# Keeping split weights in DRAM and loading them whole in later groups of a hybrid encoder step

## The chip, the cores and the metric

The kernel runs on one core of a Trainium2 chip. The metric is the device time of one execution in microseconds (us), given as the median of several runs. Engines are named as the profile names them: PE (TensorE, its weight loads apart as PEld), DVE (VectorE), ACT (ScalarE), POOL (GpSimd) and SP (SyncE, which here issues nearly all DMAs).

## The reference, cut to what matters

Two layers are applied to 2048 prompt tokens and to 8 x 16 sample tokens. Each layer is one combined projection, two mixers (A, windowed attention; B, a gated linear attention), an output projection and a gated per-layer embedding.

```
u  = rms_norm(h) @ w_in            # split into qa, ka, va, ga, qb, kb, vb, gb, ab
oa = window attention of rope(norm(qa)), rope(norm(ka)), va     # with sinks
ob = gated linear attention of qb, kb, vb, gates from ab
mix = concat(oa * silu(ga), rms_norm(ob) * silu(gb))
h  = h + mix @ w_out
h  = h + sigmoid(rms_norm(h) @ w_pg) * (p_l @ w_pe)
```

All data are float32. The weights of a layer are the same for every token.

## The kernel before

**Groups.** The 17 tiles of 128 tokens are cut into five groups of 3, 4, 4, 3 and 3 tiles (n = 384 or 512 tokens). For each layer the five groups are gone through in turn: `phase_in` makes the projections and both mixers, `phase_out` the output projection and the gate. A group is called l0g3 for layer 0, group 3. Group 4 of each layer holds the sample tile.

**Three products for one.** A float32 matrix product is made of three matmuls on rounded operands (float32r): high x high, high x low, low x high (`mm3`, lines 394 to 404; its matmuls are L400, L401 and L402). So each weight has to be in SBUF twice, as a rounded high part and a low remainder. The high part is an ACT copy (L217), the low part a DVE subtraction (through the helper `ptt`, which is why its line is L96). This is done anew in every group, ten times over the program for groups and layers together, though the parts of one layer are the same in all five groups.

**Blocks, pieces, slots.** `plan` lists the weight blocks of a group in the order in which PE uses them: kv, q, ga0, ga1, qb, kb, vb, gb, then o0 to o3 (columns of w_out), then g0, e0, g1, e1, g2, e2, g3, e3 (w_pg and w_pe). A block is loaded in pieces of 256 KB (`w_dma`, L197, on SP's queue, into four `raw` buffers), and each piece is split by one ACT and one DVE instruction (`w_split`) into a slot. A slot of tag w is 1 MB: two pieces, high and low. There are five such slots (`RING`), so a group's 76 w-pieces go through them 38 slots one after another; the small e blocks have two slots of their own. A group has 80 pieces, the program 800.

**What sets the order.** `w_split` returns without work when all five slots are held. `freed` (called behind the matmuls of the last unit that uses a slot) gives a slot back and calls `w_split` again, and `w_ahead` does so ahead of each unit. So a slot is refilled as soon as PE has let go of its last user, in the order of `plan`. Raw pieces run four ahead of the splits. Every engine runs its instructions in the order in which the scheduler of the framework put them, so a split that waits on ACT or DVE holds back what stands behind it there. Attention and the linear attention are generators that `pump` steps between the dense units. The tail of `phase_in` is the part that is asked about below: after the last unit of block gb (L1055 to 1080 of the kernel) the linear attention of the last tiles is still open, with `gsq` (squares on ACT, L895), `gss` (their norm on POOL, L896 and L898), `on` (DVE, L901), the transposes of `on` on PE (L912), and `at` and `ke` (DVE L885, ACT L888), which PE waits for in `gla_prompt`; meanwhile PE has the first halves of o0 to o2 to do.

Of the kernel before, what the change touches and what calls it, by code (L numbers as in the profile page):

```python
# [8 lines left out]
F32 = mybir.dt.float32  # L9
# [37 lines left out]
def hybrid_step(ctx: ExitStack, tc: tile.TileContext, a: dict, o: dict):  # L47
    nc = tc.nc
    V, A, G, PE, SP = nc.vector, nc.scalar, nc.gpsimd, nc.tensor, nc.sync
# [4 lines left out]
    dram = ctx.enter_context(tc.tile_pool(name="dram", bufs=1, space=bass.MemoryType.DRAM))  # L54
# [40 lines left out]
    def ptt(out, in0, in1, op1, eng=None):  # L95
        (eng or G).tensor_tensor(out=out, in0=in0, in1=in1, op=op1)  # L96
# [45 lines left out]
    plan = []  # L142
    for l in range(DEPTH):
        for gi in range(len(GROUPS)):
# [8 lines left out]
            for b in range(4):  # L153
                plan.append((l, gi, f"g{b}", 8, [a["w_pg"][l, :, b]], 4, "w"))
                plan.append((l, gi, f"e{b}", 2, [a["w_pe"][l, :, b]], 2, "we"))
    RING = dict(w=5, we=2)
    pieces = []
    for bi, (_, _, _, K, srcs, ks, _) in enumerate(plan):
        for k0 in range(0, K, 2):
            c0 = 0  # L160
            for src in srcs:
                wd = src.shape[2]
                pieces.append((bi, k0 // ks, k0 % ks, c0, wd, src[:, k0:k0 + 2, :]))
                c0 += wd
    first_piece = {}
    last_piece = {}
# [6 lines left out]
    st = dict(dma=0, split=0, blk=0)  # L173
    wgate = [None]
    RAW = Z["raw"]
# [17 lines left out]
    def w_dma(upto):  # L193
        while st["dma"] < min(upto, len(pieces)):
            bi, _, _, _, wd, src = pieces[st["dma"]]
            r = w_p.tile([128, 2, wd], F32, tag="raw", name="raw", bufs=RAW)
            SP.dma_start(out=r, in_=src)  # L197
            raws[st["dma"]] = r
            st["dma"] += 1

    def w_split():
        i = st["split"]
        if i >= len(pieces):
            return False
        bi, si, kk, c0, wd, _ = pieces[i]
        _, _, _, _, srcs, ks, tag = plan[bi]
        if (bi, si) not in slots:
            if held[tag] == RING[tag]:
                return False
            held[tag] += 1  # L210
            slots[bi, si] = w_p.tile([128, 2, ks, sum(x.shape[2] for x in srcs)], F32R, tag=tag, name="w", bufs=RING[tag])
        w_dma(i + RAW)
        w = slots[bi, si]
        r = raws.pop(i)
        hi, lo = (w[:, x, kk:kk + 2, c0:c0 + wd] for x in range(2))
        with tc.issue_after(wgate[0]) if wgate[0] is not None else ExitStack():
            A.activation(out=hi, in_=r, func=ACTF.Copy)  # L217
        ptt(lo, r, hi, ALU.subtract, V)
        st["split"] += 1
        w_dma(i + 1 + RAW)  # L220
        return True

    def w_get(l, gi, nm):
        bi = st["blk"]
        assert plan[bi][:3] == (l, gi, nm), (plan[bi][:3], l, gi, nm)
        while st["split"] <= last_piece[bi]:
            assert w_split()
        st["blk"] += 1
        return Block(bi)

    def w_get_part(l, gi, nm):

        bi = st["blk"]
        assert plan[bi][:3] == (l, gi, nm), (plan[bi][:3], l, gi, nm)
        while st["split"] < first_piece[bi] + 2:
            assert w_split()
        st["blk"] += 1
        return Block(bi)

    def w_rest(w):  # L240
        while st["split"] <= last_piece[w.bi]:
            assert w_split()
# [95 lines left out]
    def prep_x(pool, l, gi, slot, out, whole=False):  # L338
# [6 lines left out]
        if whole:  # L345
            full = pool.tile([128, KD, n], F32, tag="hfull", name="hfull", bufs=1)
            for k in range(0, KD, 2):
                HQ[k // 2].dma_start(out=full[:, k:k + 2, :], in_=src[:, k:k + 2, t0:t0 + n])
                if k // 2 in WD:
                    w_dma(WD[k // 2])  # L350
# [85 lines left out]
    def phase_in(l, gi, ip, xn, mslot, S_in):  # L436
# [651 lines left out]
        for mt in range(4):  # L1088
            if mt == 3:
                with tc.issue_after(lastmm[0]):  # L1090
                    done["tail"]()
            pss.append(unit_a(mixes, ws[mt // 2], mt % 2, 0, n, pm(n) if mt < 2 else pw1(n), ks=(0, 4), end=mt % 2 == 1))
        ws.append(w_get_part(l, gi, "o2"))
        for mt in (4, 5):
            pss.append(unit_a(mixes, ws[2], mt % 2, 0, n, pw1(n), ks=(0, 4), end=mt % 2 == 1))
# [176 lines left out]
def _prepare(inputs):  # L1272
# [65 lines left out]
    for t in range(NT):  # L1338
# [18 lines left out]
             ks=(DEPTH, 128, 128), vs=(DEPTH, 128, 128), ss=(DEPTH, 8, 128, 2, 128))  # L1357
# [32 lines left out]
```

## Time and profile before

| | |
|---|---|
| median of 3 runs | 2314.01 us (2313.35 to 2318.27) |
| the profiled execution, its own time | 2322.44 us |
| its span, first to last instruction | 2320.7 us |
| mean granted TensorE clock | 0.993 |
| PE busy | 2268.3 us, 98% |
| DVE busy | 1605.0 us, 69% |
| ACT busy | 1272.2 us, 55% |
| DMA | 278.93 MB, mean 120 GB/s |

The profiled execution is 8.4 us longer than the median of the runs. Matmuls overlap in their records (one of 384 columns lasts 0.33 us and the next starts 0.17 us after it), so "busy" says that PE always had one under way. Idle time that the profile gives for PE is time with none under way.

### The profile page before, as it was taken

How to read it: one execution, taken by the hardware profiler on the slowest of the kernel's cores; microseconds unless marked ns; L12 is line 12 of the kernel's file. 1: busy time of each engine (PE TensorE's matmuls, PEld its weight loads, DVE VectorE, ACT ScalarE, POOL GpSimd, SP SyncE). 2: the span in 40 equal slices, each digit the busy share in tenths (PEclk: the TensorE clock that was granted, in tenths of full speed). 3: DMA queues.
4: the chain of work that ended last, by engine and by line, in shares of the span. 5: the costliest groups of instructions: out<-in, count | busy, mean ns of one | idle time of the engine just before them, and what ended most of it. 6: DMA issues, size and time to landing. Idle time of an engine off the chain costs nothing.

```text
span 2320.7 us, 40960 instructions
## 1 busy us (share of the span) xinstructions
PE 2268.3 (98%) x14814; PEld 1953.6 (84%) x14814; DVE 1605.0 (69%) x3279; ACT 1272.2 (55%) x2962; POOL 671.0 (29%) x771
## 2 busy tenths in 40 slices
PE   8999999999999999999999999999999999999999
PEld 7889877887788989987988998778877888798889
DVE  7767765767567766776777677657676678677755
ACT  6555644655455645654665566445555556566533
POOL 3124322342223231413322241314412142233222
PEclk9999999999999999999999999999999999999999
DMA  5344313433154425444543543244322443264343
GB/s 159 101 150 133 107 55 119 143 105 91 55 155 120 128 85 169 147 118 127 180 128 91 171 136 90 68 128 133 114 73 74 146 146 110 85 184 146 104 131 102
DMA packets 160234, 278.93 MB, mean 120 GB/s; under 512 B 17648, under 2 KB 43632, under 8 KB 160032
## 3 DMA queue, kind: packets, MB, share of 16 engines
q1 hardware_dynamic: 159344, 275.43, 39.4%
q8 instruction: 117, 1.92, 0.3%
q10 hardware_dynamic: 688, 0.88, 0.1%
q14 instruction: 85, 0.70, 0.1%
HBM read 255.41 MB, written 20.71 MB: 119 GB/s over the span
## 4 chain that ended last, share of the span: by engine, by line
PE 83%; ACT 4%; DVE 4%; DMA 4%; issue 3%; POOL 2%; ACTq 0%; DVEq 0%; POOLq 0%; SPq 0%
PE mm L400 15%; PE mm L402 15%; PE mm L401 14%; PE pw L400 9%; PE pw L401 9%; PE pw L402 9%; PE o L131 3%; DVE w L96 2%; PE s L131 2%; PE s L125 2%; DMA raw<-in_w_pe_dram 1%; DMA raw<-in_w_out_dram 1%; PE o L125 1%; ACT gsq L895 1%; ACT w L217 1%
## 5 line engine op out<-in xcount | busy, mean ns | idle before, releaser
L96 DVE TENSOR_TENSOR w<-raw,w 128x512 fp32r<-128x512 f32 (+1 forms) x800 | 571.7, 743 | 164.6 <-ACT w L217 161.7
L217 ACT ACTIVATE w<-raw 128x512 fp32r<-128x512 f32 (+1 forms) x800 | 468.9, 627 | 271.1 <-DMA raw<-in_w_pe_dram 60.0
L96 POOL TENSOR_TENSOR ot<-gth,hst 128x384 f32<-128x384 f32 (+1 forms) x79 | 101.7, 1291 | 287.6 <-DVE gth L1189 263.4
L400 PE MATMUL mm<-B,w 128*128 128x384 f32 (+1 forms) x440 | 160.8, 365 | 1.1 <-DVE yq L470 0.8
L402 PE MATMUL mm<-B,w 128*128 128x384 f32 (+1 forms) x440 | 159.8, 363 | 0.0
L401 PE MATMUL mm<-B,w 128*128 128x384 f32 (+1 forms) x440 | 159.0, 361 | 0.0
L400 PE MATMUL pw<-mix,w 128*128 128x384 f32 (+1 forms) x424 | 153.0, 361 | 0.0
L580 ACT ACTIVATE P<-s,mx 128x192 f32<-128x192 f32 (+3 forms) x272 | 108.8, 413 | 77.5 <-DVE mx L575 71.3
L401 PE MATMUL pw<-mix,w 128*128 128x384 f32 (+1 forms) x424 | 151.2, 357 | 0.0
L402 PE MATMUL pw<-mix,w 128*128 128x384 f32 (+1 forms) x424 | 151.0, 356 | 0.0
L400 PE MATMUL mm<-A,w 128*128 128x384 f32 (+1 forms) x408 | 148.5, 364 | 2.0 <-DVE yq L470 1.8
L96 POOL TENSOR_TENSOR acc<-sq,acc 128x384 f32<-128x384 f32 (+1 forms) x60 | 74.1, 1235 | 257.1 <-ACT sq L331 257.1
L402 PE MATMUL mm<-A,w 128*128 128x384 f32 (+1 forms) x408 | 148.0, 363 | 0.0
L401 PE MATMUL mm<-A,w 128*128 128x384 f32 (+1 forms) x408 | 147.8, 362 | 0.0
L400 PE MATMUL mm<-w,A 128*128 128x512 f32 (+1 forms) x360 | 138.2, 384 | 0.0
L400 PE MATMUL mm<-w,B 128*128 128x512 f32 (+1 forms) x360 | 137.9, 384 | 0.0
L402 PE MATMUL mm<-w,B 128*128 128x512 f32 (+1 forms) x360 | 137.7, 383 | 0.0
L402 PE MATMUL mm<-w,A 128*128 128x512 f32 (+1 forms) x360 | 137.6, 382 | 0.0
L401 PE MATMUL mm<-w,A 128*128 128x512 f32 (+1 forms) x360 | 137.4, 382 | 0.0
L401 PE MATMUL mm<-w,B 128*128 128x512 f32 (+1 forms) x360 | 137.4, 382 | 0.0
L96 POOL TENSOR_TENSOR mix<-ga_t,mix 128x512 fp32r<-128x512 f32 x34 | 43.9, 1290 | 283.1 <-ACT mix L606 283.1
L1186 ACT ACTIVATE gth<-gth 128x384 f32<-128x384 f32 (+2 forms) x81 | 45.1, 560 | 125.6 <-DVE gth L1185 125.3
(325 smaller groups left out, 6367.6 us busy)
## 6 DMA issues: line engine op xcount, KB each, us to landing
raw<-in_w_in_dram SPq DMA_DIRECT2D x400, 256.0 KB, 2.9
raw<-in_w_out_dram SPq DMA_DIRECT2D x160, 256.0 KB, 3.1
raw<-in_w_pg_dram SPq DMA_DIRECT2D x160, 256.0 KB, 2.9
raw<-in_w_in_dram SPq DMA_DIRECT2D x40, 272.0 KB, 3.2
raw<-in_w_pe_dram SPq DMA_DIRECT2D x40, 256.0 KB, 3.4
hl<-in_h_dram SPq DMA_DIRECT2D x24, 192.0 KB, 3.1
hbuf<-ot SPq DMA_DIRECT2D x24, 192.0 KB, 2.1
hx<-hbuf SPq DMA_DIRECT2D x24, 192.0 KB, 3.6
```

Source lines behind the costliest of these rows:

```text
L96: (eng or G).tensor_tensor(out=out, in0=in0, in1=in1, op=op1)
L125: prev[0] = PE.matmul(**kw).ins
L131: prev[0] = PE.matmul(**kw).ins
L217: A.activation(out=hi, in_=r, func=ACTF.Copy)
L400: PE.matmul(out=out, lhsT=sh, rhs=mh, start=first and i == 0, stop=False)
L401: PE.matmul(out=out, lhsT=sh, rhs=ml, start=False, stop=False)
L402: lastmm[0] = PE.matmul(out=out, lhsT=sl, rhs=mh, start=False, stop=last and i == n).ins
L580: A.activation(out=P[:, e, p0:p0 + wd], in_=ps[:, e // 2, e % 2, :wd], func=ACTF.Exp, scale=0.125, bias=mx[:, e:e + 1], accum_out=den[:, 0 ...
L895: A.activation(out=gq, in_=po[:, h % 2, h // 2, :], func=ACTF.Square, accum_out=ss[:, h:h + 1])
L1186: ta = A.activation(out=th[:, c], in_=th[:, c], func=ACTF.Tanh, scale=0.5)
```

## The change

Two lists name blocks that are kept. The slots of ga1, qb, kb and vb are split as before in group 0 of each layer, and each finished slot (high and low, 1 MB) is then stored to a DRAM tile of its own. In groups 1 to 4 these blocks have no pieces and no split: each slot is filled by one DMA of 1 MB from that tile, issued by SP when `w_split` reaches the slot. For o1, o2, o3 and g0 the store is made in group 1 and the whole load in groups 2 to 4. All other blocks (kv, q, ga0, gb, o0, g1 to g3, e0 to e3) stay as they were. The line numbers of the changed kernel are 19 to 20 higher from the second half on; its splits are L234 and L96, its raw loads L209, its whole loads L227 and its stores L239.

```
+    KEEP = [('ga1','qb','kb','vb'),('o1','o2','o3','g0')]
+    kept = {}
+    for bi, (l, gi, nm, K, srcs, ks, _) in enumerate(plan):
+        if gi < len(KEEP) and nm in KEEP[gi]:
+            kept[l, nm] = (gi, dram.tile([K // ks, 128, 2, ks, sum(x.shape[2] for x in srcs)], F32, name=f"k{l}{nm}"))
     pieces = []
-    for bi, (_, _, _, K, srcs, ks, _) in enumerate(plan):
+    for bi, (l, gi, nm, K, srcs, ks, _) in enumerate(plan):
+        if (l, nm) in kept and gi > kept[l, nm][0]:
+            pieces += [(bi, si, 0, 0, 0, kept[l, nm][1][si]) for si in range(K // ks)]
+            continue
...
@@ w_dma
             bi, _, _, _, wd, src = pieces[st["dma"]]
+            if not wd:
+                st["dma"] += 1
+                continue
...
@@ w_split
         w = slots[bi, si]
+        if not wd:
+            SP.dma_start(out=w.bitcast(F32), in_=src)
+            st["split"] += 1
+            w_dma(i + 1 + RAW)
+            return True
...
         st["split"] += 1
         w_dma(i + 1 + RAW)
+        if kept.get((l_, nm_), (None,))[0] == gi_ and (i == last_piece[bi] or pieces[i + 1][1] != si):
+            SP.dma_start(out=kept[l_, nm_][1][si], in_=w.bitcast(F32))
```

In `w_get_part` the number of pieces that have to be split before block o2 may begin is one instead of two where the block is loaded whole.

How the instructions stand before and in the changed kernel, at three places of l0g3. In the rows `w<-raw` is a split, `raw<-in_w_in_dram`, `raw<-in_w_out_dram`, `raw<-in_w_pg_dram` and `raw<-in_w_pe_dram` are raw pieces of w_in, w_out, w_pg and w_pe, `hl` and `hx` are loads of h, `pr` of p, `th` belongs to the gate of gb, and `phl` opens `phase_out`.

ACT at the tail of `phase_in`, before:

```order
L888 ACTIVATE ke<-s 128x256
L217 ACTIVATE w<-raw 128x512 x5
L751 ACTIVATE th<-mm,cols 128x512
L217 ACTIVATE w<-raw 128x512 x3
L895 ACTIVATE gsq,gss<-o 128x128 x4
L914 ACTIVATE mix_8877<-t,vec 128x4x128
L888 ACTIVATE ke<-s 128x256
L217 ACTIVATE w<-raw 128x512 x2
L895 ACTIVATE gsq,gss<-o 128x128 x4
L914 ACTIVATE mix_8877<-t,vec 128x4x128 x2
L217 ACTIVATE w<-raw 128x512 x2
L1139 ACTIVATE phl<-pr 128x2x384
```

The same place in the changed kernel:

```order
L907 ACTIVATE ke<-s 128x256
L770 ACTIVATE th<-mm,cols 128x512
L234 ACTIVATE w<-raw 128x512 x2
L914 ACTIVATE gsq,gss<-o 128x128 x4
L933 ACTIVATE mix_8641<-t,vec 128x4x128
L907 ACTIVATE ke<-s 128x256
L770 ACTIVATE th<-mm,cols 128x512
L914 ACTIVATE gsq,gss<-o 128x128 x4
L933 ACTIVATE mix_8641<-t,vec 128x4x128 x2
L1158 ACTIVATE phl<-pr 128x2x384
```

Between one `ke` and `phl` twelve splits stood in ACT's row; two are left, those of the second half of o0.

SP from the last raw pieces of w_in to the loads of `phase_out`, before:

```order
L197 DMA raw<-in_w_in_dram 128x512 x34
L197 DMA raw<-in_w_out_dram 128x512 x16
L1132 DMA pr<-in_p_dram 128x2x384
L1136 DMA hl<-in_h_dram 128x384 x2
L356 DMA hx<-in_h_dram 128x384 x4
```

The same stretch in the changed kernel, up to the raw pieces of w_pg:

```order
L209 DMA raw<-in_w_in_dram 128x512 x8
L227 DMA w<-k0ga_92 128x2048
L209 DMA raw<-in_w_in_dram 128x512
L227 DMA w<-k0ga_92 128x2048
L209 DMA raw<-in_w_in_dram 128x512
L227 DMA w<-k0qb 128x2048 x2
L227 DMA w<-k0kb 128x2048 x2
L227 DMA w<-k0vb 128x2048 x4
L209 DMA raw<-in_w_in_dram 128x512 x4
L209 DMA raw<-in_w_out_dram 128x512 x4
L209 DMA raw<-in_w_pe_dram 128x512
L209 DMA raw<-in_w_pg_dram 128x512 x2
```

Ten whole loads have taken the place of twenty raw pieces. Each of them waits on PE for its slot, where a raw piece waited on DVE for its buffer; the first four pieces of gb stand ahead of most of them, the last four behind all.

SP behind that, from the whole loads of o1 into `phase_out`, in the changed kernel:

```order
L227 DMA w<-k0o_96 128x2048
L209 DMA raw<-in_w_pg_dram 128x512 x2
L227 DMA w<-k0o_96 128x2048
L227 DMA w<-k0o_97 128x2048 x2
L1151 DMA pr<-in_p_dram 128x2x384
L1155 DMA hl<-in_h_dram 128x384 x2
L375 DMA hx<-in_h_dram 128x384
L227 DMA w<-k0o_98 128x2048
L375 DMA hx<-in_h_dram 128x384 x3
L227 DMA w<-k0o_98 128x2048
L1155 DMA hl<-in_h_dram 128x384
L227 DMA w<-k0g_99 128x2048
```

The loads of h, which stood together, now have whole loads of o3 and g0 between them.

## Rows read from the trace of the kernel before

**Rows 1.** The page: busy us of each engine, share of the span, instructions.

```profile
PE 2268.3 (98%) x14814; PEld 1953.6 (84%) x14814; DVE 1605.0 (69%) x3279; ACT 1272.2 (55%) x2962; POOL 671.0 (29%) x771
```

**Rows 2.** PE's waits: who waited for whom, us in total, times, longest.

```profile
PE t L912 <- DVE on L901: 9.2, 13, 1.9
PE o L125 <- ACT ke L888: 7.0, 6, 2.4
```

**Rows 3.** The page's costliest groups: busy, mean ns of one, idle before and releaser.

```profile
L96 DVE TENSOR_TENSOR w<-raw,w 128x512 fp32r<-128x512 f32 (+1 forms) x800 | 571.7, 743 | 164.6 <-ACT w L217 161.7
L217 ACT ACTIVATE w<-raw 128x512 fp32r<-128x512 f32 (+1 forms) x800 | 468.9, 627 | 271.1 <-DMA raw<-in_w_pe_dram 60.0
```

**Rows 4.** Timeline, tail of l0g3 on ACT, POOL, PE: start, us, what, [idle before].

```profile
869.27 0.63 ACT L217 ACTIVATE w<-raw 128x512 fp32r<-128x512 f32 x1 [2.75 <-DMA raw<-in_w_out_dram]
...
873.17 0.26 ACT L895 ACTIVATE gsq<-o 128x128 f32<-128x128 f32 x1
...
875.27 1.01 POOL L898 TENSOR_TENSOR gss<-gss,mhalf 128x4 f32<-128x4 f32 x1
...
878.28 0.49 PE L125 MATMUL o<-vb,at 128*128 128x128 f32 x2 [2.36 <-ACT ke L888]
```

**Rows 5.** PE's waits in the tails of l0g2, l0g4, l1g2, l1g3, l1g4.

```profile
PE o L125 <- ACT ke L888: 0.6, 1, 0.6
...
PE t L912 <- DVE on L901: 2.7, 3, 1.9
...
PE o L125 <- ACT ke L888: 0.8, 1, 0.8
...
PE o L125 <- ACT ke L888: 1.7, 1, 1.7
...
PE t L912 <- DVE on L901: 4.1, 3, 1.8
```

**Rows 6.** Timeline, tail of l0g4 on POOL and PE.

```profile
1089.08 1.04 POOL L898 TENSOR_TENSOR gss<-gss,mhalf 128x4 f32<-128x4 f32 x1
...
1090.65 0.50 PE L912 MATMUL t<-cst,on 128*128 128x128 f32 x2 [1.87 <-DVE on L901]
```

**Rows 7.** Timeline where block q ends, l0g2 (529 us) and l1g4 (2130 us).

```profile
521.68 3.12 POOL L467 TENSOR_SCALAR qrs<-qrs,cols 128x8 f32<-128x8 f32 x1 [6.64 <-DVE qrs L466]
...
531.99 0.50 PE L400 MATMUL mm<-A,w 128*128 128x512 f32 x1 [1.85 <-DVE yq L470]
...
2121.53 0.44 POOL L467 TENSOR_SCALAR qrs<-qrs,cols 128x8 f32<-128x8 f32 x1
...
2132.59 0.40 PE L125 MATMUL s<-kT,qs 64*128 64x192 f32 x1 [2.23 <-issue]
```

**Rows 8.** Windows: stretch, busy us by engine, then granted clock, DMA share, GB/s.

```profile
531.00:536.00 5.00, 4.01 (x11) 3.04 (x12) 4.71 (x13) 1.02 (x4) 0.14 (x1) 0.66 0.52 166
```

**Rows 9.** The page's DMA part: queue; issues with KB each, us to landing.

```profile
q1 hardware_dynamic: 159344, 275.43, 39.4%
...
raw<-in_w_in_dram SPq DMA_DIRECT2D x400, 256.0 KB, 2.9
...
hx<-in_h_dram SPq DMA_DIRECT2D x16, 192.0 KB, 3.5
...
pr<-in_p_dram SPq DMA_DIRECT2D x4, 512.0 KB, 4.6
s<-in_s_dram SPq DMA_DIRECT2D x4, 512.0 KB, 4.0
```

**Rows 10.** The DMA burst at the start of l0g3's phase_out: issues, and its window.

```profile
hx<-in_h_dram SPq DMA_DIRECT2D x4, 192.0 KB, 4.2
...
886.00:894.00 8.00, 8.00 (x48) 8.00 (x47) 4.48 (x7) 3.34 (x6) 0.00 (x0) 1.00 0.85 272
```

**Rows 11.** Timeline of PE, l0g3: kb's first half ends, vb's fourth slot begins.

```profile
817.18 0.33 PE L402 MATMUL mm<-B,w 128*128 128x384 f32 x1
...
825.29 0.39 PE L400 MATMUL mm<-w,B 128*128 128x512 f32 x1
```

More of the change, by code (lines that the diff above doesn't have):

```diff
@@ L204, in w_split @@
             return False
-        bi, si, kk, c0, wd, _ = pieces[i]
-        _, _, _, _, srcs, ks, tag = plan[bi]
+        bi, si, kk, c0, wd, src = pieces[i]
+        l_, gi_, nm_, _, srcs, ks, tag = plan[bi]
         if (bi, si) not in slots:
@@ L234, in w_get_part @@
         assert plan[bi][:3] == (l, gi, nm), (plan[bi][:3], l, gi, nm)
-        while st["split"] < first_piece[bi] + 2:
+        while st["split"] < first_piece[bi] + (2 if pieces[first_piece[bi]][4] else 1):
             assert w_split()
```

## The prediction

> **What bounds the kernel now.** The busy shares come first: PE has a matmul under way for 2268.3 of 2320.7 us, DVE is busy for 69% and ACT for 55% [rows 1]. So a change that takes work from DVE and ACT alone can only win where PE stands still for one of them, at most 52.4 us in all. The second view is the list of PE's waits: its two largest entries are the transposes of `on`, which wait for DVE (9.2 us, 13 times), and the first product of `o`, which waits for `ke` on ACT (7.0 us, 6 times) [rows 2]. Both belong to the tail of phase_in. The third view is each such stretch on the engines that end the wait, the fourth the granted clock behind it, and the last the DMA rows, for what the change adds.
>
> **What is removed.** Kept blocks have 20 pieces (ga1, qb, kb: 4 each; vb: 8) in 4 groups and 16 (o1, o2, o3, g0) in 3 groups, in 2 layers: 2 x (4 x 20 + 3 x 16) = 256 of 800 pieces. All splits take DVE 571.7 us and ACT 468.9 us [rows 3], so DVE loses 256/800 x 571.7 = 183 us and ACT 150 us. By itself that is worth nothing, since PE's matmuls hide it; what counts is where a split stands ahead of something that PE waits for.
>
> *Tails of phase_in, groups 2 to 4 of both layers.* In l0g3 ACT goes through four splits, and stands for 2.75 us ahead of the first because its raw piece has not landed; only at 873.17 come the squares `gsq`, then POOL's `gss`, `on`, `at` and `ke`, and PE stands for 2.36 us [rows 4]. In the changed order two splits, both of o0, stand ahead of this `gsq`. The chain behind the squares is as long as before but starts about 3 us earlier, which covers the 2.36 us. The main wait of each of the six tails: 0.6 (l0g2), 2.4, 2.7 (l0g4), 0.8, 1.7 and 4.1 us (l1g4), together 12.3 [rows 4, 5]. Not all goes: in l0g4 a wait of 1.87 us ends just after `gss` comes from POOL at 1089.08 + 1.04, with no split that delays it [rows 6], and the longest wait of l1g4, 1.8 us [rows 5], is of the same kind. These two stay: 12.3 - 3.7 = 8.6 us are gained. Bounds: 4.1 (only the two waits for `ke` in the groups 3) and 12.3.
>
> *End of q in l0g2 and l1g4.* In l0g2 PE waits 1.85 us for `yq`, which needs `qrs` from POOL; the L467 there took 3.12 us, where the same instruction took 0.44 us at 2121 [rows 7]. DVE was splitting while it ran. Of the splits at this place only those of ga0 remain, since ga1 and qb come whole. In l1g4 PE waits 2.23 us [rows 7] while ACT has splits of the same blocks ahead of the copy that PE needs. I take both as gained, 4.1 us; bounds 0 and 4.1.
>
> *The clock.* Behind the wait in l0g2 the granted clock (the number after the five engines) has a mean of 0.66 over 5 us [rows 8]: the lower of its two levels, 1.2 GHz, for two thirds of that, 3.4 us, after PE stood still. Half speed for 3.4 us costs 1.7 us. With both waits gone the like behind l1g4's goes too: 3.4 us; bounds 0 and 3.4.
>
> **What is added.** Whole loads of 1 MB: 2 x (4 x 10 + 3 x 8) = 128, in the place of 64 MB of raw pieces; stores of 1 MB: 2 x 18 = 36. With 1.05 MB (10^6) for each, DMA goes from 279 to 279 + 67 + 38 = 384 MB, or from 39.4% of the DMA engines [rows 9] to some 54%. That mean binds nothing. What matters is the moment: a slot that PE lets go must be full before PE needs it again.
>
> No load of 1 MB is in this trace. 256 KB lands 2.9 us after its issue, 512 KB after 4.0 (`s`) or 4.6 (`pr`) [rows 9]. At 1.1 or 1.7 us for each further 256 KB, 1 MB takes 4.0 + 2 x 1.1 = 6.2 or 4.6 + 2 x 1.7 = 8.0 us. I take 6.2: `s` comes alone, as the whole loads do, `pr` at the head of a burst. That burst moved 272 GB/s over 8 us [rows 10], at which the 0.79 MB beyond 256 KB take 2.9 us, which would give 5.8.
>
> The tightest slot is the fourth of vb. It follows the first half of kb, whose last matmul ends at 817.18 + 0.33 in l0g3; its own first matmul starts at 825.29 [rows 11], 7.8 us later. Counted in the same way, the eight groups with whole loads of vb have 7.7 to 10.5 us, three of them under 8; every other kept slot has over 11. So 6.2 us, and some tenths for semaphore and issue, fit with a us to spare; at 8.0 us three groups would wait some 0.5 us. I charge 0.5 us; bounds 0 and 2.
>
> Among the whole loads stand `hl` and `hx`. A load behind 1 MB lands some 3 us later. `hl` is needed two units of 12 matmuls later (4.2 us), so the third to fifth of eight come late; PE does not wait for them, since the last two units have 24 matmuls each and make this up. I charge 1 us; bounds 0 and 3.
>
> Stores in groups 0 and 1 stand on SP behind raw pieces that are already four ahead. Raw pieces issued after a store land about 3 us later, and ACT, which waits for them, then holds back the tail. Four groups, 0 to 3 us in each; I take 1 in each group 1, where the stores of o1 and o2 meet the tail, and 0.5 in each group 0: 3 us, bounds 0 and 12.
>
> **Sum.** Gained 8.6 + 4.1 + 3.4 = 16.1, lost 0.5 + 1 + 3 = 4.5, net 11.6 us. The profiled execution, 2322.4 us, would come to 2310.8; it stands 8.4 us above the median of the runs, which would be 2314.0 - 11.6, or **2302.5 us**. A measurement of this kernel can tell about 0.2%, 4.6 us, from no change.
>
> **Rivals.**
>
> 1. *Given back, no change.* The tails wait for POOL and for the length of the chain rather than for splits, and the stores cost more than I charge. Then the lower 4.1 us come from the tails, 2 us from the ends of q, nothing from the clock, and 6 are lost: 2314. For it: some 1 us of `gss` sits in each of these chains [rows 4, 6]. Against: in l0g3 ACT stood for 2.75 us on one raw piece alone. That the scheduler fills the places with other work (the change would not do what it says) would look the same; ACT's rows in the changed order speak against that.
>
> 2. *Slower: vb comes late.* A whole load waits on SP for PE, and what stands behind it waits too. If 1 MB takes L us from the release to landing, PE waits L - 7.8 us in three groups and about L - 10 in five. At L = 13 that is 3 x 5.2 + 5 x 3 = 31 us against 12.1 of gain that is left after the other two costs: 2333. It decides from L just under 11, where 3 x 3.0 + 5 x 0.8 = 13 us cancel the gain. For it: loads of 192 KB that were issued four in a row needed 4.2 us against 3.5 in the median [rows 9, 10], so loads queue behind one another. The Trainium skill (DMA: Bandwidth & Descriptors, HWDGE ordering) has it that what SP issues goes through one ring on each DMA engine, consumed in ring order; by that rule a load behind two of 1 MB lands some 6 us late, and L would be 12. The trace agrees in kind, with the 0.7 us just named; no run here shows a load behind one of 1 MB. Against: the slots ahead of vb's fourth are let go several us earlier, so little should be in flight when it is issued.
>
> 3. *More is gained, since POOL is freed too.* If POOL is held up by splits, as 3.12 against 0.44 us suggests [rows 7], then `qrs` and `gss` come earlier wherever splits went: the two waits that I let stay halve (2 us), their stretches at 1.2 GHz go (3.4 us), and the costs of 4.5 us drown in the slack: 2302.5 - 9.9 = 2293. The Trainium skill states such a rule (SBUF — State Buffer, on the shared port pair): a DVE instruction with two SBUF inputs and a GpSimd instruction that reads SBUF shut each other out for the whole instruction. The trace agrees at this one place, with the 3.12 us.
>
> **Chances.** The forecast has 0.51, with 2297 to 2309 as its own range; rival 3 has 0.12; rival 1, within 4.6 us of 2314, 0.22; rival 2, or the stores at their upper bound (12 us for 3 cancels most of the gain and with a late vb more than that), 0.15. So faster by over 0.2% has 0.63, within 0.2% 0.22, slower 0.15. The range of 2292 to 2317 holds the forecast, most of rival 3 and rival 1, and leaves out the slower case.
>
> **What would show it.** Right: DVE busy near 1605 - 183 = 1422 us and ACT near 1122; PE's wait for `ke` down from 7.0 to under 3 us; no wait near 1.8 us for `yq` where q ends in l0g2; whole loads that land in 6 to 7 us; PE's idle time down by about 10 us. Wrong: PE waiting for a DMA from the kept tiles (`k0vb`, `k1vb`); waits for `ke` and `on` in groups 2 to 4 as long as before; longer tails in groups 0 and 1; a median within 4.6 us of 2314.

## The result, and the profile after

| | before | changed |
|---|---|---|
| median (5 runs each, same chip) | 2315.4 us | 2304.5 us |
| lowest to highest | 2313.4 to 2318.3 | 2302.4 to 2305.7 |
| ratio, 95% interval | | 0.9944 [0.9932, 0.9955] |
| profiled execution, its span | 2322.4, 2320.7 us | 2302.4, 2300.6 us |
| mean granted clock of it | 0.993 | 0.997 |

The change is faster. The medians differ by 10.9 us; the ratio in the table, which is not the quotient of the two medians, gives 13.0 us (10.4 to 15.7). The two profiled executions lie 20.1 us apart: that of before was 7 us slower than its own median, and that of the change was the fastest of its five. What follows therefore leans on two profiles of each kernel.

The page of the changed kernel: busy us and share of the span (answers to [rows 1]).

```profile
PE 2258.1 (98%) x14814; PEld 1946.8 (85%) x14814; DVE 1445.9 (63%) x3023; ACT 1135.2 (49%) x2706; POOL 647.5 (28%) x771
```

PE now stands idle for 2300.6 - 2258.1 = 42.5 us instead of 52.4. The rest of the 20.1 us is mostly the clock. The granted clock stood at 1.2 GHz for 30.7 us of the span before and for 15.4 us now, which at half speed is some 8 us.

PE's waits (who for whom; us in total, times, longest), which answer to [rows 2]:

```profile
PE t L931 <- DVE on L920: 6.1, 9, 1.9
PE pw L419 <- DVE gth L1204: 4.5, 5, 1.6
...
PE o L125 <- ACT ke L907: 1.6, 2, 0.8
```

The waits for `ke` and `on`, in the tails of phase_in, went from 16.2 to 7.7 us on these lines, and to 9.0 us with two small entries that are new (`o` for `on`, 1.0 us; `s` for `ke`, 0.3 us). The second line is new as a large entry: the same wait had 2.5 us in the profile of before. It is in phase_out, and no term of the forecast was priced for it.

The split groups of the page (busy, mean ns of one, idle before) and, from the DMA view, the queue of SP, whole loads and loads of h (answer to [rows 3] and [rows 9]):

```profile
L96 DVE TENSOR_TENSOR w<-raw,w 128x512 fp32r<-128x512 f32 (+1 forms) x544 | 403.8, 767 | 130.8 <-ACT w L234 126.7
L234 ACT ACTIVATE w<-raw 128x512 fp32r<-128x512 f32 (+1 forms) x544 | 319.6, 627 | 178.7 <-DMA raw<-in_w_pe_dram 44.3
```

```profile
q1 hardware_dynamic: 146096, 380.28, 48.7%
w<-k0vb SPq DMA_DIRECT2D x16, 1024.0 KB, 4.8
w<-k0g SPq DMA_DIRECT2D x6, 1024.0 KB, 6.0
hl<-in_h_dram SPq DMA_DIRECT2D x24, 192.0 KB, 3.8
```

Of 800 splits 256 are gone, as forecast, and SP's queue holds 48.7% of the DMA engines' time (54 were forecast). Whole loads of `vb`, on which rival 2 rests, land in 4.8 us in the median, others in up to 7.4 us (`k1g`), and PE waits for no kept tile anywhere. `hl` took 3.1 us in the median before and takes 3.8 now.

The tail of l0g3, on ACT and PE (start, us, what, [idle before]; answers to [rows 4]):

```profile
857.73 1.15 ACT L234 ACTIVATE w<-raw 128x512 fp32r<-128x512 f32 x2 [0.61 <-PE mm L421]
...
860.69 0.28 ACT L914 ACTIVATE gsq<-o 128x128 f32<-128x128 f32 x1 [1.81 <-PE o L131]
...
867.69 0.38 PE L125 MATMUL o<-vb,at 128*128 128x128 f32 x2
```

ACT's splits no longer wait 2.75 us for a raw piece. `gsq` starts because PE has finished its operand, not because ACT has got through its splits. PE's first product of `o` has no idle time in front of it.

### The profile page after: what moved, and what is told of

Its sections match the earlier page's. It is cut to its first block, busy times and chain, and to the rows that moved or that the text cites. A ratio compares the mean times of both kernels' runs of the same rounds, so it can differ in the third digit from the quotient of the medians.

```text
span 2300.6 us, 39902 instructions
## 1 busy us (share of the span) xinstructions
PE 2258.1 (98%) x14814; PEld 1946.8 (85%) x14814; DVE 1445.9 (63%) x3023; ACT 1135.2 (49%) x2706; POOL 647.5 (28%) x771
## 3 DMA queue, kind: packets, MB, share of 16 engines
q1 hardware_dynamic: 146096, 380.28, 48.7%
## 4 chain that ended last, share of the span: by engine, by line
PE 84%; DMA 4%; ACT 4%; DVE 3%; issue 3%; POOL 2%; ACTq 0%; DVEq 0%; POOLq 0%
PE mm L421 15%; PE mm L419 15%; PE mm L420 15%; PE pw L419 8%; PE pw L421 8%; PE pw L420 8%; PE o L131 4%; DMA raw<-in_w_pe_dram 2%; PE s L131 2%; PE s L125 2%; DVE w L96 1%; PE o L125 1%; POOL xacc L96 1%; PE t L131 1%; PE t L931 1%
## 5 line engine op out<-in xcount | busy, mean ns | idle before, releaser
L96 DVE TENSOR_TENSOR w<-raw,w 128x512 fp32r<-128x512 f32 (+1 forms) x544 | 403.8, 767 | 130.8 <-ACT w L234 126.7
L234 ACT ACTIVATE w<-raw 128x512 fp32r<-128x512 f32 (+1 forms) x544 | 319.6, 627 | 178.7 <-DMA raw<-in_w_pe_dram 44.3
L96 POOL TENSOR_TENSOR ot<-gth,hst 128x384 f32<-128x384 f32 (+1 forms) x79 | 101.7, 1291 | 294.6 <-DVE gth L1208 270.0
L96 POOL TENSOR_TENSOR acc<-sq,acc 128x384 f32<-128x384 f32 (+1 forms) x60 | 71.4, 1190 | 257.2 <-ACT sq L350 256.9
L96 POOL TENSOR_TENSOR mix<-ga_t,mix 128x512 fp32r<-128x512 f32 x34 | 44.0, 1295 | 267.7 <-ACT mix L625 267.7
```

## The experiments

| run | edit | median us | ratio to before [95%] |
|---|---|---|---|
| after_again | the change | 2306.2 | 0.9949 [0.9936, 0.9962] |
| keep_first | ga1, qb, kb, vb alone | 2302.4 | 0.9924 [0.9911, 0.9937] |
| keep_second | o1, o2, o3, g0 alone | 2313.2 | 0.9975 [0.9965, 0.9984] |
| stores_only | stored, never loaded | 2319.8 | 1.0007 [0.9998, 1.0017] |
| dummy_both | first list, ACT and DVE work put back | 2326.3 | 1.0042 [1.0029, 1.0055] |
| dummy_act | ... ACT's alone | 2318.5 | 1.0006 [0.9997, 1.0015] |
| dummy_dve | ... DVE's alone | 2329.6 | 1.0060 [1.0047, 1.0073] |
| o1o2 | first list, o1, o2 | 2300.8 | 0.9933 [0.9921, 0.9946] |
| no_g0 | first list, o1, o2, o3 | 2303.5 | 0.9935 [0.9921, 0.9948] |
| gb_o0_too | as o1o2, and gb, o0 | 2295.2 | 0.9901 [0.9887, 0.9914] |
| ga0_too | as gb_o0_too, and ga0 | 2296.9 | 0.9908 [0.9889, 0.9926] |
| before_again | the kernel before, one run | 2321.4 | |

The kernel before had medians of 2317.7 to 2319.6 us beside these runs, which were made on four chips. The ratios are better compared than the medians; they are again not quotients of the medians, and their intervals are 2 to 4 parts in a thousand wide, so differences of less than that between two rows are not told by them.

### How far one profile can be trusted

The change and the kernel before were profiled once more.

> The changed kernel once more, for the spread of a profile by stage. If the stretches at 1.2 GHz went because of the change, this profile too has at most one of them between 50 and 2290 us, and phase_out again waits 4 to 5 us for gth; if they come and go by chance, it has several. Time 2303 to 2306 us.

> The kernel before once more, with a profile: which of its stages differ between two executions. If the 2.4 us at the end of l0g0 and the 3 to 6 us where q ends in l1g0, which the change does not touch, were chance in the first profile, they are 1 us or more smaller in at least one of the two places here; the waits of the tails of the groups 3 (2.4 and 1.7 us) and the wait for yq in l0g2 (1.85 us) should be the same within 0.3 us. Stretches at 1.2 GHz after 50 us: four to six, if they belong to this kernel.

The wait of l0g3's tail in the second profile of before (PE, start, us, [idle before]):

```profile
876.93 0.49 PE L125 MATMUL o<-vb,at 128*128 128x128 f32 x2 [2.61 <-ACT ke L888]
```

The waits on which the forecast rests come back: 2.61 us here (2.36 in [rows 4]) and 1.83 us for `yq` in l0g2 (1.85); the wait of l1g3's tail grew from 1.71 to 2.08 us, a little more than the 0.3 us expected. The wait where q ends in l1g0 was 3.4 us in the first profile and 1.9 in this one. Those 1.5 us are chance and no part of the change. The end of l0g0 did not get shorter: it is 2 us longer in both profiles of before than in stores_only (run below). All three have a wait of 2.2 us for `ah` there, but behind it both profiles of before have a stretch at 1.2 GHz and stores_only has none; the rest is the wait for `gth` (1.4 and 0.8 us against 0.3).

Between 50 and 2290 us there are 6 and 7 stretches at 1.2 GHz in the two profiles of before (four to six were expected), and none in either profile of the change. That overstates the difference: both profiles of the change are the fastest of their runs, with a mean granted clock of 0.997, and the other runs of the change go down to 0.994. So these stretches are rarer in the change, not gone. The waits for `gth` at L1204 vary: 5.8 us in the first profile of the change (4.5 and 1.3 on two lines), 2.7 in the second, where 4 to 5 were expected.

### Which list does it

```diff
-    KEEP = [('ga1','qb','kb','vb'),('o1','o2','o3','g0')]
+    KEEP = [('ga1','qb','kb','vb'),()]
```

> Only ga1, qb, kb and vb are kept; o1 to o3 and g0 are split in every group. My theory (splits that stand ahead of the tails and of the ends of q): this part has the ends of q and the clock, 4.1 + 3.4 us less 1.5 for stores, vb and h, so about 6 us below before (2309), with no wait of 1.8 us where q ends in l0g2 and the waits for ke of the two groups 3 still at 1.5 us or more each. Rival (time comes from the load on POOL and DVE as a whole, wherever the split stands): 160 of the 256 kept pieces, so 160/256 of the 11 us, 7 us, and the waits for ke get shorter too. Rival (all comes from the tails): 2314 to 2317.

```diff
-    KEEP = [('ga1','qb','kb','vb'),('o1','o2','o3','g0')]
+    KEEP = [(),('o1','o2','o3','g0')]
```

> Only o1, o2, o3 and g0 are kept; ga1, qb, kb and vb are split in every group. My theory: this part has the tails, 8.6 us less 2 to 3 for the stores in the groups 1 and for h, so about 6 us below before (2309); the waits for ke of the groups 3 are gone, the wait of some 1.8 us where q ends in l0g2 is there. Rival (load as a whole): 96/256 of 11 us, 4 us. Rival (all comes from the first list): 2314 to 2317.

```diff
-        if (l, nm) in kept and gi > kept[l, nm][0]:
+        if False:
```

> The kept blocks are stored as in the change, but every block is split in every group; nothing is loaded whole. So this gives the price of the 36 stores alone. My theory: 1 to 3 us above before (2316 to 2318), in the groups 0 and 1. Rival (stores are free): within 1 us of before. Rival (stores cost what the bound allowed): up to 12 us, 2327.

The first list alone is at least as fast as the whole change (2302.4 against 2304.5 and 2306.2). The second alone gives about half of the change's gain. So the lists do not add up: 0.76% and 0.25% apart, 0.51 to 0.56% together. For the first list every theory was too low: 15.3 us were gained, 6 and 7 had been expected. For the second, 4.4 us by the medians and 5.8 by the ratio do not tell the load as a whole (4) from mine (6). In stores_only the intervals leave the price of the stores between nothing and 3.9 us, 1.6 in the middle.

PE's waits in keep_second, the end of q in l0g2 and the first product that needs `gth` in l0g3:

```profile
530.84 0.67 PE L419 MATMUL mm<-A,w 128*128 128x512 f32 x1 [1.84 <-DVE yq L489]
...
925.34 0.45 PE L419 MATMUL mm<-B,w 128*128 128x384 f32 x1 [1.31 <-DVE gth L1204]
```

The end of q is the first list's, as forecast. The long waits in the tails of the groups 3 go with either list: PE does not wait there at all in keep_first, where they were expected to stay, and 0.50 us in keep_second. That is a reason why the gains overlap. The second list brings the waits for `gth`: 3.2 and 1.3 us in keep_second, 0.2 and 0.2 in keep_first.

### What in a split holds the tails back: ACT, DVE or the raw piece

The first list alone, with the work of each missing split put back on constants. In the variants one of the two lines is left out, and DVE then subtracts `cst[:, 128:640]` from `cst[:, :512]`.

```diff
+                for j in range(ks // 2 * len(srcs)):
+                    pieces.append((bi, si, 0, j, 0, kept[l, nm][1][si]))
...
+                raws[st["dma"]] = w_p.tile([128, 512], F32, tag="raw", name="raw", bufs=RAW)
...
-            SP.dma_start(out=w.bitcast(F32), in_=src)
+            if not c0:
+                SP.dma_start(out=w.bitcast(F32), in_=src)
+            r = raws.pop(i)
+            A.activation(out=r, in_=cst[:, :512], func=ACTF.Copy)
+            ptt(r, cst[:, :512], r, ALU.subtract, V)
```

> Only ga1, qb, kb and vb are kept (2302.4 us, 15.3 below before), and for each of their 160 pieces that is no longer split ACT copies a constant of 128x512 into a raw buffer and DVE subtracts in place there, at the place in the program where the split stood; the buffer waits for no DMA and no weight slot. Those results are thrown away. Theory A (the time that splits take of ACT and DVE ahead of the chains counts): most of the gain goes, 2311 to 2317, the wait for yq where q ends in l0g2 is back at 1 us or more. Theory B (only the wait of the split for its raw piece counts): the gain stays, 2302 to 2305.

> The same with the copies on ACT alone. If ACT's time ahead of the chains counts, half or more of the gain goes (2308 or more); if the raw pieces, DVE or POOL count, it stays within 2 us of 2302.4.

> The same with the subtractions on DVE alone (two SBUF inputs, 128x512). If POOL is held up while DVE subtracts, POOL's L486 goes from 0.49 us in the mean back to 0.7 or more, the wait for yq in l0g2 is back, and half or more of the gain goes (2308 or more); if ACT or the raw pieces count, it stays within 2 us of 2302.4, with L486 at 0.5.

None of these waits for the DMA of its own piece, and all three lose the whole gain. Theory B (the raw piece's own wait) falls. By the totals ACT's copies would count as well as DVE's subtractions, but two of the three end above before, so the totals overstate it: a dummy waits for no weight slot, and waits at the start of q grow. In dummy_act the waits of `pw` for `abT` come to 10.4 us in five, where before has 3.4 us in three, and four of its six stretches at 1.2 GHz after 50 us stand at waits for `abT`. The places tell more than the totals.

dummy_dve in l0g2 and l0g3 (POOL's `qrs` as in [rows 7]; ACT's first split of the tail and PE's `o` as in [rows 4]):

```profile
522.16 3.72 POOL L492 TENSOR_SCALAR qrs<-qrs,cols 128x8 f32<-128x8 f32 x1 [7.01 <-DVE qrs L491]
...
866.95 0.63 ACT L240 ACTIVATE w<-raw 128x512 fp32r<-128x512 f32 x1 [2.70 <-DMA raw<-in_w_out_dram]
...
875.64 0.49 PE L125 MATMUL o<-vb,at 128*128 128x128 f32 x2 [1.95 <-ACT ke L913]
```

With DVE's subtractions alone, the old tail is back, down to ACT's wait of 2.70 us for a raw piece of w_out (2.75 in [rows 4]); in l1g3 PE waits 1.87 us. At the end of q in l0g2 PE waits 1.15 us for `yq`, so that wait is back in part. The raw piece is late because its buffer comes free late: SP's queue waits for DVE's subtractions (`SPq L212 <- DVE w L96`) before it can issue it. In the kernel before it is the same. There ACT is through with its four splits at 866.52, SP can issue the next piece only at 866.48, when the first of these four subtractions ends, and it lands 2.7 us later:

```profile
865.77 3.28 DVE L96 TENSOR_TENSOR w<-raw,w 128x512 fp32r<-128x512 f32 x4
...
866.48 6.76 SPq L197 DMA_DIRECT2D raw<-in_w_out_dram  x7
```

dummy_act at the same two places; PE has no idle time in the tails of l0g3 and l1g3:

```profile
525.92 1.24 POOL L492 TENSOR_SCALAR qrs<-qrs,cols 128x8 f32<-128x8 f32 x1 [6.97 <-DVE qrs L491]
...
534.08 0.47 PE L425 MATMUL mm<-A,w 128*128 128x512 f32 x1 [0.51 <-DVE yq L495]
...
868.02 1.15 ACT L240 ACTIVATE w<-raw 128x512 fp32r<-128x512 f32 x2 [0.21 <-PE mm L427]
...
869.63 0.28 ACT L920 ACTIVATE gsq<-o 128x128 f32<-128x128 f32 x1 [0.46 <-PE o L131]
```

ACT's copies alone bring back neither the tail nor the long wait at the end of q in l0g2. So the chain in a slow tail is: DVE subtracts, a raw buffer comes free, a piece lands, ACT can split, and only then come the squares.

What starts this chain is shown only in part, because the order of ACT's row differs too. Between `ke` and `gsq` in l0g3 there are eight splits in before, stores_only, dummy_both and dummy_dve, and in each of them ACT waits 2.4 to 2.9 us for a raw piece. In dummy_act and keep_first there are four, in the change and in keep_second two, and ACT waits for no raw piece. So DVE's time alone is not enough: keep_second has all subtractions of the first list and no slow tail. Why the scheduler put eight splits there in one kernel and four in another is not shown.

The same `qrs` instruction over the whole kernel, 34 times 128x8: before, changed, dummy_dve, dummy_act (busy, mean ns).

```profile
L467 POOL TENSOR_SCALAR qrs<-qrs,cols 128x8 f32<-128x8 f32 x34 | 26.0, 766 | 99.0 <-DVE qrs L466 98.2
```

```profile
L486 POOL TENSOR_SCALAR qrs<-qrs,cols 128x8 f32<-128x8 f32 x34 | 16.7, 490 | 97.0 <-DVE qrs L485 96.1
```

```profile
L492 POOL TENSOR_SCALAR qrs<-qrs,cols 128x8 f32<-128x8 f32 x34 | 39.1, 1151 | 89.9 <-DVE qrs L491 88.5
```

```profile
L492 POOL TENSOR_SCALAR qrs<-qrs,cols 128x8 f32<-128x8 f32 x34 | 14.2, 419 | 119.3 <-DVE qrs L491 118.4
```

The instruction is slow where DVE subtracts and fast where it does not, whatever ACT does. The rule of the Trainium skill (SBUF — State Buffer, SBUF: two separate sides) that a DVE operation with two SBUF inputs and a GpSimd operation that reads SBUF exclude each other agrees with these four means. One exclusion alone does not make the 3.72 us of a single `qrs` in l0g2, which is longer than five of the dummies' subtractions (0.68 us each).

### What the second list costs

```diff
-    KEEP = [('ga1','qb','kb','vb'),('o1','o2','o3','g0')]
+    KEEP = [('ga1','qb','kb','vb'),('o1','o2')]
```

> The first list, and of the second o1 and o2 alone, so that no whole load stands among the loads of h in phase_out. My theory (the second list gives 2 us in the tails of the groups 2 and costs 5 to 6 us since hl lands behind o3 and g0, hst and so gth come late): the waits for gth over 1 us at the first products of phase_out go, as in the first list alone, and the time is 2300 to 2302. Rival (what the second list costs are its stores, or its loads as such): two thirds of that cost stay for half of the blocks, 2303 to 2304.5, nearer to the change.

```diff
-    KEEP = [('ga1','qb','kb','vb'),('o1','o2','o3','g0')]
+    KEEP = [('ga1','qb','kb','vb'),('o1','o2','o3')]
```

> The change without g0 in the second list: whole loads of o3 still stand among the loads of h, those of g0 no longer. If the cost is in hl behind whole loads, some of it goes: the waits for gth over 1 us in the groups of three tiles fall from 1.1 to 1.6 us to between 0.3 and 1 us, and the time lies between o1 and o2 alone and the change, 2301 to 2303.5. Rival (what matters is the number of blocks that are still split): no change of those waits, 2304 to 2305.

SP and DVE at the start of l0g3's phase_out in the changed kernel, and PE 25 us later:

```profile
884.11 0.33 SPq L1155 DMA_DIRECT2D hl<-in_h_dram  x1
885.60 0.33 SPq L227 DMA_DIRECT2D w<-k0g  x1
886.19 3.98 SPq L1155 DMA_DIRECT2D hl<-in_h_dram  x2
...
889.26 0.56 DVE L1179 TENSOR_TENSOR hst<-pw,hl 128x384 f32<-128x384 f32 x1 [1.79 <-DMA hl<-in_h_dram]
893.25 1.07 DVE L1179 TENSOR_TENSOR hst<-pw,hl 128x384 f32<-128x384 f32 x2 [2.14 <-DMA hl<-in_h_dram]
...
919.49 0.45 PE L419 MATMUL mm<-B,w 128*128 128x384 f32 x1 [1.32 <-DVE gth L1204]
```

The same in keep_first:

```profile
884.06 2.26 SPq L1155 DMA_DIRECT2D hl<-in_h_dram  x2
...
887.82 0.55 DVE L1179 TENSOR_TENSOR hst<-pw,hl 128x384 f32<-128x384 f32 x1
...
888.39 2.10 SPq L1155 DMA_DIRECT2D hl<-in_h_dram  x2
...
889.59 0.55 DVE L1179 TENSOR_TENSOR hst<-pw,hl 128x384 f32<-128x384 f32 x1
...
918.19 0.45 PE L419 MATMUL mm<-B,w 128*128 128x384 f32 x1 [0.21 <-DVE gth L1204]
```

In the change the load issued at 886.19, behind a whole load of g0, is there for DVE only at 893.25, 7.1 us later. In keep_first `hst` starts 3.8 us after its load is issued and waits for nothing. From `hst` on the chain is in line: B and the squares, their sum, the mean by PE, `ny` and `nr`, then `gth`. So a late `hl` is paid for by PE 25 us later.

no_g0, with only o3's loads ahead of `hl`:

```profile
892.17 0.56 DVE L1179 TENSOR_TENSOR hst<-pw,hl 128x384 f32<-128x384 f32 x1 [3.51 <-DMA hl<-in_h_dram]
...
892.76 0.62 ACT L1182 ACTIVATE B<-hst,vec 128x384 fp32r<-128x384 f32 x1 [4.51 <-DVE hst L1179]
...
908.96 0.45 PE L419 MATMUL mm<-B,w 128*128 128x384 f32 x1 [0.98 <-ACT B L1182]
```

In no_g0 the long waits for `gth` are gone in layer 1 and in l0g4, but not in l0g3, where `hl` behind o3 costs PE 0.98 us for B and 1.4 for `gth`. The expectation of a fall in each group was wrong; the time, 2303.5, lies where it was expected. In o1o2, with no whole load among the loads of h, all waits for `gth` at L1204 together are 1.2 us, and the time is 2300.8. The ratios of the two runs, 0.9935 and 0.9933, do not tell them apart, and their intervals overlap with those of the change; what the second list costs is shown by the waits at their places, and by the totals only as a tendency.

By the Trainium skill (DMA: Bandwidth & Descriptors, Queues, rings and completion order), what SP issues shares one ring on each DMA engine, and descriptors are consumed in ring order. The 7.1 us behind a load of 1 MB agree with that.

### A better version

```diff
-    KEEP = [('ga1','qb','kb','vb'),('o1','o2','o3','g0')]
+    KEEP = [('ga1','qb','kb','vb','gb','o0'),('o1','o2')]
```

> A try at a better version: ga1, qb, kb, vb, gb and o0 kept from group 0, o1 and o2 from group 1. The eight waits of 0.8 to 1.9 us that are left in the tails (ke in the groups 1, on in l0g4 and l1g4) have splits of gb and o0 beside them. If DVE's subtractions are what still holds these chains, they shorten and the time is 2295 to 2299; if the chains are as long as they must be (POOL and ACT in line), it stays at 2300 to 2302; if the whole loads of gb come late for their slots, PE waits for a kept tile and it is above 2303.

```diff
-    KEEP = [('ga1','qb','kb','vb'),('o1','o2','o3','g0')]
+    KEEP = [('ga0','ga1','qb','kb','vb','gb','o0'),('o1','o2')]
```

> The better version with ga0 kept as well. If DVE's subtractions still hold the end of q in l1g4 (0.34 and 1.07 us are left there), those waits go and the time is 2293 to 2295; if the whole loads of ga0 come late behind q, PE waits there for a kept tile and it is 2297 or more.

gb_o0_too is faster than both kernels: 2295.2 us, 0.9901 against 0.9944 and 0.9949 for the change, with intervals that do not touch (that of keep_first it just overlaps). Against o1o2 PE stands idle for 34.0 instead of 39.0 us. Its whole loads of gb (5.4 us) and of o (7.9 us) come in time.

```profile
w<-k0o SPq DMA_DIRECT2D x20, 1024.0 KB, 7.9
w<-k0gb SPq DMA_DIRECT2D x16, 1024.0 KB, 5.4
```

Its tails of the groups 1 and of l0g4:

```profile
386.57 0.46 PE L125 MATMUL o<-vb,at 128*128 128x128 f32 x2 [0.35 <-ACT ke L907]
...
1073.40 0.28 ACT L914 ACTIVATE gsq<-o 128x128 f32<-128x128 f32 x1 [4.79 <-PE o L131]
...
1077.50 1.01 PE L931 MATMUL t<-cst,on 128*128 128x128 f32 x4 [1.86 <-DVE on L920]
```

The wait for `ke` in l0g1 falls from 0.81 to 0.35 us, and in l1g1 it goes. The 1.86 us in l0g4 stay to the hundredth with hardly a split left beside them: that chain is as long as it is, as the prediction had it. ga0_too is no faster. Its wait for `yq` in l1g4 is 1.40 us, so it was not ga0's splits that were left there.

How long PE waits for this chain is another matter. From the first of the four squares to the transposes it takes 4.1 us in before, the change, gb_o0_too and ga0_too alike. Yet in ga0_too PE waits only 0.96 us in l0g4, and in the change only 0.99 us at the like place of l1g4:

```profile
1072.98 0.28 ACT L914 ACTIVATE gsq<-o 128x128 f32<-128x128 f32 x1 [4.20 <-PE o L131]
...
1077.08 1.01 PE L931 MATMUL t<-cst,on 128*128 128x128 f32 x4 [0.96 <-DVE on L920]
```

```profile
2213.35 0.28 ACT L914 ACTIVATE gsq<-o 128x128 f32<-128x128 f32 x1 [4.20 <-PE o L131]
...
2217.45 0.76 PE L931 MATMUL t<-cst,on 128*128 128x128 f32 x3 [0.99 <-DVE on L920]
```

What differs is the number of dense matmuls that PE has to do meanwhile: 11 where it waits 1.86 us, 16 in these two. Five more at 0.17 us each are the 0.9 us.

## Why the prediction was right, term by term

The forecast was 2302.5 us; 2304.5 and 2306.2 were measured, within its own range. That the sum was so close is in part luck, for errors of both signs cancelled: the tails and the ends of q gave less than forecast and `hl` cost as much or more, while the clock gave more and the stores and `vb` cost less.

| term | forecast | shown |
|---|---|---|
| tails, groups 2 to 4 | +8.6 | 12.3 us of main waits became 4.7: +7.6 |
| end of q, l0g2 and l1g4 | +4.1 | 4.1 us became 0 and 1.4: +2.7 |
| clock | +3.4 | +5.3 |
| vb's fourth slot | -0.5 | 0 |
| hl and hx behind 1 MB | -1 | -0.9 and -3.0 (waits for `gth`, two pairs of profiles) |
| stores | -3 | -1.6 (-3.9 to +0.5) |
| sum | 11.6 | 11.0 to 13.1; measured 10.9 and 11.5 (medians), 13.0 and 11.8 (ratios) |

**Tails.** The step held, with the size and the two waits that were to stay. What remains in the tails that were counted:

```profile
PE t L931 <- DVE on L920: 2.8, 2, 1.9
...
PE t L931 <- DVE on L920: 1.9, 2, 1.0
```

The first row is l0g4, the second l1g4. The reason given, splits on ACT ahead of the squares with one raw piece late, fits too: the slow tails are those with eight splits there. What the prediction did not have is DVE's part, which lets the raw buffer go and so makes the piece late, and which blocks bring the gain: the author gave the long waits of the groups 3 to the second list, and the first alone removes them.

**End of q.** l0g2 went as forecast. For l1g4 the step "I take both as gained" was too much: PE still waits 0.34 us for `qs` and 1.08 for `yq`, and ga0_too shows that the splits left there are not the cause.

**Clock.** The step "with both waits gone the like behind l1g4's goes too: 3.4 us" was mis-sized. It counted two stretches, those behind the ends of q. The other four or five of before stand behind other waits, of tails, of phase_out and of q in l1g0. Not all of these waits went: those of 2.2 us for `ah` in l0g0 and of 1.86 us in l0g4 are as long in the change, and it is chance that no stretch follows them in its two profiles, since ga0_too has a stretch behind the first of them and o1o2 behind the second. Over all runs the mean granted clock is 0.9937 before (23 runs) and 0.9960 in the change (11 runs): 0.0023 of 2316 us, 5.3 us, or three stretches in an average run; six in the pair of profiles first compared. At the 1.4 us that a stretch costs where it was measured (last section), three are 4.3 us.

**vb, and rival 2.** A whole load of vb lands in 4.8 us against the 6.2 that were taken, and no wait of PE names a kept tile. Rival 2 needed nearly 11. A load does wait behind a whole load, as `hl` shows, and so does the third of vb, which is issued some 2 to 3 us before the second has landed and takes up to 7.9 us. But when the fourth, the tight one, is issued, no whole load is in flight any more, and in all eight groups it lands in 4.6 to 5.1 us.

**hl.** Here a step failed: "PE does not wait for them, since the last two units have 24 matmuls each and make this up". It looked at the product that uses `hl` and not at the chain behind it. PE's 24 matmuls cover `hst` nearly everywhere; they do not cover `gth`. In the first profiles the waits for `gth` grew from 2.8 to 5.8 us, in the second ones from 1.8 to 2.7 (and 0.7 us for `A`, which `hst` feeds, is new there); keep_first has 0.4. By medians the second list costs 2 to 4 us on top of the first, with intervals that still overlap.

**Rivals 1 and 3.** Rival 1 is false: the tails gave 7.6 us. Rival 3 is half right. POOL's `qrs` is freed (766 to 490 ns), but `gss` at L917 takes 1.01 us as before, and of the two waits left in place one stays at 1.86 us while the other falls from 1.84 to 0.99. That is not POOL's doing: the chain behind the squares takes 4.1 us at both places as before, and PE has 16 matmuls beside it in l1g4 where it had 11.

**Signs.** DVE's busy time was forecast at 1422 us and is 1445.9. Of these 24 us, about 15 come from the splits that are left, most of it since they take longer, 762 ns for 128x512 (738 before); 9 are other work of DVE. No run was made for the cause of that.

## What to carry to other kernels

When work is taken off two engines that fill a buffer in turn, ask which of them lets the buffer in front of it go: that one sets when the next transfer starts, even when the idle time stands on the other. Look also at how many pieces stand in a row ahead of the chain that matters: with four buffers, the tails with eight of them were slow here and those with four were not. A wait for a chain of fixed length shrinks when the waiting engine has more to do beside it, with nothing taken off the chain. A large load is paid for by what is queued behind it, so its place in the queue counts more than its bytes; follow a small load that it delays to the end of its chain, not to its first use. Two parts of a change that shorten the same wait do not add up, and the cheaper one should be tried alone.

## What the runs showed of the hardware

Every stretch at 1.2 GHz between 50 and 2285 us, 44 in 14 profiles, began within some 2 us of the end of a wait of PE of 1.4 us or more, mostly behind it and sometimes still in it, and lasted 3.4 or 6.8 us. But a wait does not always bring one: 36 of 64 waits of 1.8 us or more had a stretch, 7 of 27 between 1.5 and 1.8, 3 of 51 between 1.0 and 1.5. The same wait of 1.86 us in l0g4's tail was followed by full clock in the change (first) and by a stretch in o1o2 (second). The granted clock stands behind the five engines, and PE's rows are the transposes that end the wait and the first dense product behind them:

```profile
1080.00:1085.00 5.00, 3.81 (x32) 3.13 (x33) 2.48 (x7) 1.69 (x7) 0.66 (x1) 1.00 0.62 211
...
1081.19 1.01 PE L931 MATMUL t<-cst,on 128*128 128x128 f32 x4 [1.86 <-DVE on L920]
...
1084.27 0.44 PE L419 MATMUL pw<-mix,w 128*128 128x384 f32 x1
```

```profile
1080.00:1085.00 5.00, 4.52 (x29) 3.71 (x29) 1.86 (x5) 1.03 (x3) 0.00 (x0) 0.66 0.50 195
...
1080.48 1.16 PE L931 MATMUL t<-cst,on 128*128 128x128 f32 x4 [1.86 <-DVE on L920]
...
1084.98 0.45 PE L419 MATMUL pw<-mix,w 128*128 128x384 f32 x1
```

The same work took 3.08 us at full clock and 4.50 with the stretch, 1.4 us more (the forecast had 1.7). So a wait of 1.8 us or more costs its own time and, about every second time, some 1.4 us besides. Executions with a lower mean clock are also the longer ones: of the 11 runs of keep_second the one at 0.993 took 2318.3 us, and the five at 0.996 and 0.997 took 2306.9 to 2313.2 us.

The dummies showed how much one engine can slow another that it shares no data with: POOL's 128x8 `qrs` in l0g2 took 1.24 us in dummy_act and 3.72 us in dummy_dve.
